# Queries and keys of a retention head projected by token, rotated there and turned by eight transposes

## The chip, the cores and the metric

The kernel runs on one core of a Trainium2 chip. The metric is the device time in microseconds of one execution, less is better. A core has a matrix engine (TensorE, in the profile PE, with its weight loads as PEld), a vector engine (VectorE, DVE), a scalar engine (ScalarE, ACT), GpSimd (POOL) and SyncE (SP), which here issues the DMAs. Matrix products are written to PSUM, of which the kernel uses eight banks of 128 partitions by 512 float32; everything else lies in SBUF.

## The reference

Two decoder layers over 256 tokens of width 2048, in float32. Each layer is a token mixer and a SwiGLU network, each with a root-mean-square norm, a shift and scale before it and a gate behind it that come from a conditioning vector through `w_mod`. The first layer's mixer is retention, the second's a short gated convolution. The change touches the retention alone:

```python
q, k, v, g = jnp.split(h @ w_in, [qk_w, 2 * qk_w, 2 * qk_w + v_w], axis=-1)
q = rope(split_heads(q, RET_HEADS), cos, sin)
k = rope(split_heads(k, RET_HEADS), cos, sin) * (RET_DK ** -0.5)
o = rms_norm(chunked_gated_linear_attention(q, k, v, log_a))
return ((jax.nn.silu(g) * o) @ w_out).astype(h.dtype)

def rope(t, cos, sin):
    half = t.shape[-1] // 2
    t1, t2 = t[..., :half], t[..., half:]
    return jnp.concatenate([t1 * cos - t2 * sin, t2 * cos + t1 * sin], axis=-1)
```

There are 8 heads. A head's queries and keys are 256 wide each, its values and its gate 512 each. The angle of `rope` is the token's position times one of 128 frequencies.

## The kernel before

**Precision.** Every float32 operand of a product is split into a high part, rounded to the matrix engine's faster float32 format, and a low part, the rest. A product is three matmuls: high by high, high by low, low by high. Weights come by DMA in pieces of 128 x 2048 (`fetch`, L291), of which each half of 1024 columns is rounded by ScalarE (L310) and subtracted by VectorE (L313). `laid_out` writes all weights into one array in the order in which the kernel uses them, and `take` hands them out in that order.

**Two forms of projection.** The hidden rows `h` lie transposed, 16 row tiles of 128 features by 256 tokens. In `packed` an item of 128 weight columns makes the weights stationary and streams the 256 tokens past them: three matmuls of 256 columns (L395 to L397), and the result has features on the partitions. An item of 512 columns goes to `by_token`: for each half of the tokens `h` is stationary and the 512 weight columns stream, three matmuls (L370 to L372), and the result has tokens on the partitions. Before the change q and k of a head are two items of 128 columns each, values and gate one item of 512. I call the work of one head and one row tile a step. A unit, by which `ticked` and `paced` count, is 128 weight columns of one row tile.

**The start.** While the modulation of the first norm is still coming in (32 loads of 1 MB, each reduced on VectorE, L656), q, k and gate are projected for five heads as far as rows of `h` are ready: `SPANS` lists the heads and row tiles, 60 steps in all. Two heads at a time fill the eight banks, and unfinished sums are put aside in SBUF (`held`, ScalarE L643 or VectorE L640). The last span, head 4, stays in its banks. In this part VectorE's and ScalarE's order is written by hand; the sines and cosines of the angles (`angles`) are made in between.

**The heads.** `projections` goes through the heads in the order 4, 0, 2, 1, 5, 3, 6, 7: the rest of q, its rotation on VectorE (`rope`, L822 to L826), the split into high and low (L828, L829), the same for k, then the values (`values`), the scores (`scores`, L857 and L860), the gate. What needs the scores is put on a list, `asides`, as pairs of a number of units and a piece of work: after 8 units of the next projection the first half of the outputs (L884), after 8 more the second half with its norm, after 20 more the eight transposes of the outputs (`ends`, L904), which turn them to features on partitions. The order on TensorE is the order in the program. On VectorE and ScalarE a scheduler orders the heads' work. `paced` lets go of the remaining modulation sums (L244, one pass of VectorE over 128 x 2048), after each group of projections up to two. In the middle and at the end of the heads stands a part of the output projection (`ret_out`).

**The norm behind.** The later norms read rows of `x`, scaled, from the same buffer as `h`, `raw_all`, with two columns more in front of each row for the shift (L528 to L530). Each row tile has a pitch of 514 columns there.

Of the kernel before, what the change touches and what calls it, by code (L numbers as in the profile page):

```python
# [10 lines left out]
F32 = mybir.dt.float32  # L11
F32R = mybir.dt.float32r
# [5 lines left out]
P = 128  # L18
# [26 lines left out]
MOD_PRIO = -300  # L45
STEPS = (8, 8, 20)
RAW_BUFS = 3
PART_BUFS = 4
LEFT, ENDS, EARLIER = 8, 2, 120

# [82 lines left out]
def in_use_order():  # L133

    for g in RET_SPANS:
        yield "ret_w_in", 0, g
    for n, h in enumerate(HEAD_ORDER):
        qkg, v = RET_HEADS[h]
        for g in qkg[:2] + [v] + qkg[2:]:
            yield "ret_w_in", 0, g  # L140
        if n % (HEADS // 2) == HEADS // 2 - 1:
            for g in RET_OUT[n // (HEADS // 2)]:
                yield "ret_w_out", 0, g
    for layer in range(DEPTH):
        if layer == 1:
            for g in CONV_IN:
                yield "conv_w_in", 0, g
            for g in CONV_OUT:
                yield "conv_w_out", 0, g
        for part in range(2):  # L150
            for g in FFN_IN[part]:
                yield "ffn_w_in", layer, g
            for g in FFN_OUT[part]:
                yield "ffn_w_out", layer, g


def laid_out(arrays):
# [4 lines left out]
    for key, i, g in in_use_order():  # L162
        for k in g.ks:
            for c, w in g.items:
                o = at % CHUNK
                out[at // CHUNK, :, o : o + w] = arrays[key][i, k * P : (k + 1) * P, c : c + w]
                at += w
    assert at == total and total % CHUNK == 0
# [7 lines left out]
def table():  # L176
# [9 lines left out]
def trunk(ctx: ExitStack, tc: tile.TileContext, x_in, c_in, pos_in, w_mod, cols_in, tab_in, w_all, out):  # L186
# [307 lines left out]
    h = rows_at(EARLIER)  # L494
    raw_all = h_all.rearrange("p (k n) -> p k n", k=KT + 1)[:, :KT, :]

    def scaled_only(layer, norm, j):

        needed(layer, SC2 if norm else SC1, j)
        a = mod_a[layer][norm][:, j : j + 1]  # L500
        high, low = raw_all[:, j, ENDS : ENDS + S], raw_all[:, j, ENDS + S :]
        nc.scalar.activation(high, x[j], AF.Identity, scale=a)
        nc.vector.scalar_tensor_tensor(low, x[j], a, high.bitcast(F32), op0=ALU.mult, op1=ALU.subtract)

    def normed(accs, layer, norm, g):
# [18 lines left out]
        for k in g.ks:  # L524
            high, low = raw_all[:, k, : ENDS + S], raw_all[:, k, ENDS + S :]
            for c, pt in zip(g.cols, banks):
# [53 lines left out]
    with ExitStack() as inner:  # L580
        rm = inner.enter_context(tc.tile_pool(name="rmid", bufs=1))

        def angles():

            both = rm.tile([P, 2, S], I32, tag="mid17", name=name("angles"))
            pos, ang = both[:, 0, :], both[:, 1, :].bitcast(F32)
            nc.sync.dma_start(pos, pos_in.to_broadcast([P, S]))
            magic = 1.5 * 2.0**23
# [8 lines left out]
            parts.append(rest)  # L597
            k = pos.bitcast(F32)
# [26 lines left out]
            ]  # L625

        sin = rm.tile([P, S], F32, tag="sin", name="sin")
        cos = rm.tile([P, S], F32, tag="cos", name="cos")
# [16 lines left out]
        with tc.tile_pool(name="start", bufs=1) as sp:  # L645
# [59 lines left out]
            with tc.manual_schedule(engines={mybir.EngineType.DVE, mybir.EngineType.Activation}):  # L705
# [6 lines left out]
                loaded(SH1, 0)  # L712
                nc.sync.dma_start(tab, tab_in[:, : 1 + P])
                fetch()
# [103 lines left out]

        def rope(s, tag, ours):

            a = tmp("qa", (P, 2, S), pool=rp, bufs=1)
            nc.vector.tensor_tensor(a, s, cos.unsqueeze(1).to_broadcast([P, 2, S]), op=ALU.mult)  # L822
            b = s if ours else tmp("qs", (P, 2, S), pool=rp, bufs=1)
            nc.vector.tensor_tensor(b, s, sin.unsqueeze(1).to_broadcast([P, 2, S]), op=ALU.mult)
            nc.vector.tensor_tensor(a[:, 0, :], a[:, 0, :], b[:, 1, :], op=ALU.subtract)
            nc.vector.tensor_tensor(a[:, 1, :], a[:, 1, :], b[:, 0, :], op=ALU.add)  # L826
            dst = rp.tile([P, 2, 2, S], F32R, tag=tag, name=name(tag))
            nc.scalar.copy(dst[:, 0, :, :], a)  # L828
            nc.vector.tensor_tensor(dst[:, 1, :, :], a, dst[:, 0, :, :].bitcast(F32), op=ALU.subtract)  # L829
            return dst  # L830

# [14 lines left out]

        def scores(head, q, k):
            decay = rp.tile([P, S], F32, tag="decay", name=name("decay"), bufs=1)
            nc.sync.dma_start(decay, tab_in[:, 1 + P + head * S : 1 + P + (head + 1) * S])
            both = []  # L850
            for jt in range(2):
# [16 lines left out]
                both.append(sp)  # L868
            return both

# [42 lines left out]

        def pair(head, i):

            g = RET_HEADS[head][0][i]
            if not g.ks:
                return [ahead[head, n] for n in ((i,) if i < 2 else (2, 3))]
            sums = packed(g, h)
            for j, pt in enumerate(sums):  # L920
                key = (head, i + j)
                if key in tag_of:
                    free.append(tag_of.pop(key))
                if key in ahead:
                    s = tmp("qs", (P, 2, S), pool=rp, bufs=1)
                    nc.vector.tensor_tensor(s, ahead[key], pt, op=ALU.add)
                    sums[j] = s
            return sums
# [150 lines left out]
```

## Time and profile before

| | us |
|---|---|
| median of the runs | 2627.57 (2622.59 to 2627.66) |
| the profiled execution | 2620.08 |
| its span, first to last instruction | 2618.3 |
| TensorE busy | 2592.6 |
| VectorE busy | 1991.1 |
| ScalarE busy | 1253.4 |
| first matmul of the projections | 19.43 |
| end of the spans | 202.27 |
| first part of the output projection | 348.87 |
| second part of the output projection | 686.87 |

A row of the groups reads: line, engine, operation, tile written <- tiles read, shapes, count, then busy time and mean duration of one, then the idle time of the engine before them and what ended it. A row of the timeline has the start and the duration of one instruction or of several alike. Matmuls overlap: the distance from one start to the next is what one costs, not the duration shown. A wait's row has the total in microseconds, how often, and the longest.

### The profile page before, as it was taken

How to read it: one execution, taken by the hardware profiler on the slowest of the kernel's cores; microseconds unless marked ns; L12 is line 12 of the kernel's file. 1: busy time of each engine (PE TensorE's matmuls, PEld its weight loads, DVE VectorE, ACT ScalarE, POOL GpSimd, SP SyncE). 2: the span in 40 equal slices, each digit the busy share in tenths (PEclk: the TensorE clock that was granted, in tenths of full speed). 3: DMA queues.
4: the chain of work that ended last, by engine and by line, in shares of the span. 5: the costliest groups of instructions: out<-in, count | busy, mean ns of one | idle time of the engine just before them, and what ended most of it. 6: DMA issues, size and time to landing. Idle time of an engine off the chain costs nothing.

```text
span 2618.3 us, 38264 instructions
## 1 busy us (share of the span) xinstructions
PE 2592.6 (99%) x15248; PEld 2305.3 (88%) x15248; DVE 1991.1 (76%) x2528; ACT 1253.4 (48%) x1791; POOL 141.8 (5%) x225
## 2 busy tenths in 40 slices
PE   7999999999999999999999999999999999999998
PEld 6898889888899888888888898888998888888888
DVE  7988878887698877777777889888887665555554
ACT  5544543444456444344444454444554443444443
POOL 0000000110000010110100001100000000000000
PEclk9999999999999999999999999999999999999999
DMA  9976668777686877777777768777677665555553
GB/s 397 390 288 224 250 250 304 291 260 275 243 306 247 329 290 278 270 287 289 288 267 281 272 224 324 288 277 270 256 272 267 251 224 193 192 186 186 192 193 129
DMA packets 96375, 687.58 MB, mean 263 GB/s; under 512 B 10690, under 2 KB 12098, under 8 KB 13250
## 3 DMA queue, kind: packets, MB, share of 16 engines
q1 hardware_dynamic: 96194, 685.13, 70.6%
q8 instruction: 119, 1.95, 0.3%
q14 instruction: 62, 0.50, 0.1%
HBM read 682.99 MB, written 2.10 MB: 262 GB/s over the span
## 4 chain that ended last, share of the span: by engine, by line
PE 75%; issue 20%; DVE 2%; DMA 2%; ACT 1%; DVEq 0%; POOLq 0%; POOL 0%; ACTq 0%
PE bank L355 34%; PE bank L358 18%; PE bank L370 4%; PE bank L371 4%; PE bank L372 4%; PE bank L397 2%; PE bank L396 2%; PE bank L395 2%; PE bank L528 1%; PE bank L530 1%; PE bank L529 1%; DMA raw<-w_all 1%; DVE raw L656 1%; DVE lo L313 1%; PE bank L884 1%
## 5 line engine op out<-in xcount | busy, mean ns | idle before, releaser
L313 DVE TENSOR_TENSOR lo<-raw,hi 128x1024 fp32r<-128x1024 f32 x912 | 1112.0, 1222 | 539.9 <-ACT hi L310 538.2
L310 ACT CAST hi<-raw 128x1024 fp32r<-128x1024 f32 x912 | 953.8, 1050 | 1075.6 <-PE bank L355 633.2
L355 PE MATMUL bank<-h,hi 128*128 128x512 f32 x3296 | 1142.9, 390 | 0.0
L358 PE MATMUL bank<-h,lo 128*128 128x256 f32 x3296 | 929.6, 282 | 0.0
L355 PEld LDWEIGHTS bank<-h,hi 128*128 128x128 f32 x3296 | 618.8, 188 | 129.5
L358 PEld LDWEIGHTS bank<-h,lo 128*128 128x128 f32 x3296 | 622.9, 189 | 0.2 <-DVE lo L313 0.2
L355 PE MATMUL bank<-mid,hi 128*128 128x512 f32 x1604 | 556.3, 390 | 0.0
L358 PE MATMUL bank<-mid,lo 128*128 128x256 f32 x1604 | 452.4, 282 | 0.3 <-DVE lo L313 0.3
L244 DVE SCALAR_TENSOR_TENSOR raw<-raw,cb 128x2048 f32<-128x2048 f32 x160 | 365.5, 2284 | 17.6 <-DMA raw<-w_mod 17.3
L355 PEld LDWEIGHTS bank<-mid,hi 128*128 128x128 f32 x1604 | 301.2, 188 | 63.1
L358 PEld LDWEIGHTS bank<-mid,lo 128*128 128x128 f32 x1604 | 303.2, 189 | 0.6 <-DVE lo L313 0.6
L370 PE MATMUL bank<-hi,h 128*128 128x512 f32 x512 | 201.6, 394 | 1.5 <-DVE rm L640 1.5
L371 PE MATMUL bank<-lo,h 128*128 128x512 f32 x512 | 200.4, 391 | 0.0
L372 PE MATMUL bank<-hi,h 128*128 128x512 f32 x512 | 199.6, 390 | 0.0
L355 PE MATMUL bank<-rm,hi 128*128 128x512 f32 x496 | 172.5, 390 | 0.0
L397 PE MATMUL bank<-h,lo 128*128 128x256 f32 x512 | 146.5, 286 | 4.3 <-DVE lo L313 4.3
L395 PE MATMUL bank<-h,hi 128*128 128x256 f32 x512 | 145.8, 285 | 3.3 <-ACT h L684 3.3
L396 PE MATMUL bank<-h,hi 128*128 128x256 f32 x512 | 146.0, 285 | 0.8 <-DVE h L685 0.8
L358 PE MATMUL bank<-rm,lo 128*128 128x256 f32 x496 | 139.8, 282 | 0.0
L372 PEld LDWEIGHTS bank<-hi,h 128*128 128x128 f32 x512 | 96.4, 188 | 20.7
L370 PEld LDWEIGHTS bank<-hi,h 128*128 128x128 f32 x512 | 96.8, 189 | 19.8 <-DVE rm L640 2.1
L371 PEld LDWEIGHTS bank<-lo,h 128*128 128x128 f32 x512 | 96.8, 189 | 17.3
(155 smaller groups left out, 2249.8 us busy)
## 6 DMA issues: line engine op xcount, KB each, us to landing
raw<-w_all SPq DMA_DIRECT2D x456, 1024.0 KB, 4.8
raw<-w_mod SPq DMA_DIRECT2D x192, 1024.0 KB, 5.0
x<-x_in SPq DMA_DIRECT2D x4, 512.0 KB, 5.7
out<-y SPq DMA_DIRECT2D x3, 512.0 KB, 3.6
decay<-tab_in SPq DMA_DIRECT2D x8, 128.0 KB, 3.2
out<-y SPq DMA_DIRECT2D x2, 256.0 KB, 4.5
cols<-cols_in SPq DMA_DIRECT2D x1, 160.0 KB, 8.9
angles<-pos_in SPq DMA_DIRECT2D x1, 128.0 KB, 9.6
```

The costliest lines, as they stand in the source:

```text
L244: nc.vector.scalar_tensor_tensor(raw, raw, 1.0, cb, op0=ALU.mult, op1=ALU.mult, accum_out=total)
L310: nc.scalar.copy(hi, raw)
L313: nc.vector.tensor_tensor(lo, raw, hi.bitcast(F32), op=ALU.subtract)
L355: nc.tensor.matmul(pt, hi, h, start=fresh and k == g.ks[0], stop=False, skip_group_check=True)
L358: nc.tensor.matmul(pt[:, 1, :], lo, h[:, 0, :], start=False, stop=last and k == g.ks[-1], skip_group_check=True)
L370: nc.tensor.matmul(o, ht[:, 0, :], hi, start=first, stop=False)
L371: nc.tensor.matmul(o, ht[:, 0, :], lo, start=False, stop=False)
L372: nc.tensor.matmul(o, ht[:, 1, :], hi, start=False, stop=last)
L395: nc.tensor.matmul(pt, hi, h[:, 0, :], start=first, stop=False, skip_group_check=True)
L396: nc.tensor.matmul(pt, hi, h[:, 1, :], start=False, stop=False, skip_group_check=True)
L397: nc.tensor.matmul(pt, lo, h[:, 0, :], start=False, stop=last, skip_group_check=True)
L528: nc.tensor.matmul(pt, hi, high, start=k == 0, stop=False, skip_group_check=True)
```

## The change

q and k of a head become one item of 512 columns, gathered from two places of `w_in`, so `packed` projects them through `by_token` and their tokens lie on the partitions. The rotation is done there, one call for each half of the tokens, with sines and cosines that have tokens on the partitions too; the angles are now made from the position as a scalar of each partition and a table with the frequencies in every row. Eight transposes (`turned_qk`) bring q and k of both halves into two banks with features on the partitions, where they are split as before. The turns and the scores become pieces of work on the list: the turns 32 units into the values (counted together with what is left on the list of the head before, at least 8), the scores 20 units behind them. The group of q and group of k become one, so `paced` is called once with 64 units for 2 x 32. The pitch of the rows in `raw_all` becomes 520. The rotated tile has two buffers.

```diff
+TURN_AT, SCORES_AT = 32, 20
-LEFT, ENDS, EARLIER = 8, 2, 120
+LEFT, ENDS, EARLIER, ROW = 8, 2, 120, 520
...
-        q = [Q0 + h * DK + i * P for i in range(2)]
-        k = [K0 + h * DK + i * P for i in range(2)]
-        qkg.append([q, k, [(G0 + h * DV, DV)]])
+        qkg.append([[((Q0 + h * DK, K0 + h * DK), 2 * DK)], [(G0 + h * DV, DV)]])
...
-    parts = [inv[:, None], np.eye(P), decay.transpose(1, 0, 2).reshape(P, HEADS * S)]
+    parts = [np.tile(inv, (P, 1)), np.eye(P), decay.transpose(1, 0, 2).reshape(P, HEADS * S)]
...
-    tab = const.tile([P, 1 + P], F32, tag="tab", name="tab")
-    inv_freq, ident = tab[:, 0:1], tab[:, 1 : 1 + P]
+    tab = const.tile([P, 2 * P], F32, tag="tab", name="tab")
+    inv_freq, ident = tab[:, :P], tab[:, P:]
...
-    h_all = hpool.tile([P, (KT + 1) * (ENDS + 2 * S)], F32R, tag="h", name="h")
-    hpool.tile([P, 88], F32, tag="beside", name="beside")
+    h_all = hpool.tile([P, KT * ROW], F32R, tag="h", name="h")
...
-            nc.sync.dma_start(pos, pos_in.to_broadcast([P, S]))
+            nc.sync.dma_start(pos, pos_in)
...
-                nc.vector.tensor_copy(ang, pos)
-                nc.vector.tensor_scalar(ang, ang, inv_freq, None, op0=ALU.mult)
+                nc.vector.tensor_copy(place, pos)
+                for t in range(2):
+                    at = slice(t * P, (t + 1) * P)
+                    nc.vector.tensor_scalar(ang[:, at], inv_freq, place[:, t : t + 1], None, op0=ALU.mult)
...
-        def rope(s, tag, ours):
-
-            a = tmp("qa", (P, 2, S), pool=rp, bufs=1)
-            nc.vector.tensor_tensor(a, s, cos.unsqueeze(1).to_broadcast([P, 2, S]), op=ALU.mult)
+        def rope(s, t, ours):
...
+            def whole(v):
+                return v[:, t * P : (t + 1) * P].unsqueeze(1).to_broadcast([P, 4, P])
...
+            a = tmp("qa", (P, 2, S), pool=rp, bufs=2)
+            nc.vector.tensor_tensor(parts(a), parts(s), whole(cos), op=ALU.mult)
             b = s if ours else tmp("qs", (P, 2, S), pool=rp, bufs=1)
...
+            nc.vector.tensor_tensor(parts(b), parts(s), whole(sin), op=ALU.mult)
+            (a0, a1), (b0, b1) = halves(a), halves(b)
+            nc.vector.tensor_tensor(a0, a0, b1, op=ALU.subtract)
+            nc.vector.tensor_tensor(a1, a1, b0, op=ALU.add)
+            return a
+
+        def turned_qk(both, q_and_k):
+
+            banks = [bank() for _ in range(2)]
+            for t, a in enumerate(both):
+                for n, pt in enumerate(banks):
+                    for i in range(2):
+                        nc.tensor.transpose(
+                            pt[:, i, t * P : (t + 1) * P], a[:, n, i * P : (i + 1) * P], ident
+                        )
+            for tag, pt in zip("qk", banks):
+                dst = rp.tile([P, 2, 2, S], F32R, tag=tag, name=name(tag))
+                nc.scalar.copy(dst[:, 0, :, :], pt)
+                nc.vector.tensor_tensor(dst[:, 1, :, :], pt, dst[:, 0, :, :].bitcast(F32), op=ALU.subtract)
+                q_and_k.append(dst)
...
         def projections(head):
-            q = rope(*pair(head, 0), "q", (head, 0) in ahead)
-            k = rope(*pair(head, 1), "k", (head, 1) in ahead)
+            both = pair(head, 0, rope)
+            waiting = sum(n for n, _ in asides) - since[0] if asides else 0
+            if not asides:
+                since[0] = 0
+            q_and_k, sp = [], []
+            asides.append((max(TURN_AT - waiting, STEPS[0]), lambda: turned_qk(both, q_and_k)))
+            asides.append((SCORES_AT, lambda: scores(head, *q_and_k, sp)))
             v = values(head, RET_HEADS[head][1])
-            sp = scores(head, q, k)
-            sg = [gate(s) for s in pair(head, 2)]
+            sg = pair(head, 1, lambda s, t, ours: gate(s))
+            if not asides:
+                since[0] = 0
             asides.extend(mixed(head, sp, v, sg))
-            since[0] = 0
```

More of the change, by code (lines that the diff above doesn't have):

```diff
@@ L138, in in_use_order @@
         qkg, v = RET_HEADS[h]
-        for g in qkg[:2] + [v] + qkg[2:]:
+        for g in qkg[:1] + [v] + qkg[1:]:
             yield "ret_w_in", 0, g
@@ L164, in laid_out @@
             for c, w in g.items:
-                o = at % CHUNK
-                out[at // CHUNK, :, o : o + w] = arrays[key][i, k * P : (k + 1) * P, c : c + w]
-                at += w
+                places = c if isinstance(c, tuple) else (c,)
+                for c in places:
+                    n, o = w // len(places), at % CHUNK
+                    out[at // CHUNK, :, o : o + n] = arrays[key][i, k * P : (k + 1) * P, c : c + n]
+                    at += n
     assert at == total and total % CHUNK == 0
@@ L625, in angles @@
             ]
+        pos = const.tile([P, 2], I32, tag="pos", name="pos")
+        place = const.tile([P, 2], F32, tag="place", name="place")
         sin = rm.tile([P, S], F32, tag="sin", name="sin")
@@ L712, in trunk @@
                 loaded(SH1, 0)
-                nc.sync.dma_start(tab, tab_in[:, : 1 + P])
+                nc.sync.dma_start(tab, tab_in[:, : 2 * P])
                 fetch()
@@ L845, in values, with scores @@
             return v
-        def scores(head, q, k):
+        def scores(head, q, k, both):
             decay = rp.tile([P, S], F32, tag="decay", name=name("decay"), bufs=1)
-            nc.sync.dma_start(decay, tab_in[:, 1 + P + head * S : 1 + P + (head + 1) * S])
-            both = []
+            nc.sync.dma_start(decay, tab_in[:, 2 * P + head * S : 2 * P + (head + 1) * S])
             for jt in range(2):
@@ L912, in mixed, with pair @@
             return list(zip(STEPS, [lambda: outputs(0), last_outputs, ends]))
-        def pair(head, i):
+        def pair(head, i, then):
             g = RET_HEADS[head][0][i]
+            keys = [(head, 2 * i + t) for t in range(2)]
             if not g.ks:
[L918 to L921, printed above, removed]
+                return [then(ahead[key], t, True) for t, key in enumerate(keys)]
+            out = []
+            for t, (key, pt) in enumerate(zip(keys, packed(g, h))):
+                s = pt
                 if key in tag_of:
```

29 lines of the change are left out of this document (12 added, 17 removed).

## The prediction

> **What bounds the kernel now.** I read the page's busy table and slices, then TensorE's waits, then busy time by stage, then the timeline where the two forms of projection stand side by side.
>
> ```profile
> span 2618.3 us, 38264 instructions
> PE 2592.6 (99%) x15248; PEld 2305.3 (88%) x15248; DVE 1991.1 (76%) x2528; ACT 1253.4 (48%) x1791; POOL 141.8 (5%) x225
> ...
> PEclk9999999999999999999999999999999999999999
> ```
>
> TensorE has work for 99% of the span at full granted clock. So what counts is how many matmuls it gets, how far apart they start, and where it waits; of that last there is little:
>
> ```profile
> PE bank L397 <- DVE lo L313: 4.3, 5, 1.8
> PE bank L395 <- ACT h L684: 3.3, 2, 2.5
> ...
> PE bank L370 <- DVE rm L640: 1.5, 2, 0.8
> ...
> PE bank L884 <- DVE sp L413: 0.5, 1, 0.5
> ```
>
> All but the last are in the first 128 us. By stage (columns: length, busy time and count of PE, PEld, DVE, ACT, POOL, granted clock, DMA share, GB/s):
>
> ```profile
> 19.00:128.00 109.00, 101.37 (x609) 89.80 (x609) 99.72 (x102) 61.43 (x93) 0.00 (x0) 0.98 1.00 406
> 128.00:203.00 75.00, 74.85 (x475) 67.92 (x476) 64.72 (x78) 36.66 (x49) 0.00 (x0) 1.00 0.74 279
> 225.10:687.00 461.90, 461.31 (x2586) 404.57 (x2586) 371.95 (x464) 209.07 (x285) 42.82 (x62) 1.00 0.73 267
> ```
>
> Up to 128 us the DMA engines are full (1.00) and VectorE is busy 91%, so TensorE is fed as fast as weights come and are split. From 128 us it is the bound. The stretch ends in a wait for VectorE's L640, part of an unbroken row of VectorE work:
>
> ```profile
> 127.42 0.68 DVE L640 TENSOR_TENSOR rm<-rm,bank 128x512 f32<-128x512 f32 x1
> 128.02 2.28 DVE L656 SCALAR_TENSOR_TENSOR raw<-raw,cb 128x2048 f32<-128x2048 f32 x1
> ```
>
> ```profile
> 128.15 0.50 PE L370 MATMUL bank<-hi,h 128*128 128x512 f32 x1 [0.77 <-DVE rm L640]
> ...
> 128.95 0.28 PE L395 MATMUL bank<-h,hi 128*128 128x256 f32 x1
> ...
> 199.45 0.28 PE L395 MATMUL bank<-h,hi 128*128 128x256 f32 x1
> ...
> 200.88 0.40 PE L370 MATMUL bank<-hi,h 128*128 128x512 f32 x1
> ...
> 202.27 0.39 PE L370 MATMUL bank<-hi,h 128*128 128x512 f32 x1
> ...
> 440.59 0.28 PE L395 MATMUL bank<-h,hi 128*128 128x256 f32 x1
> ...
> 463.61 0.40 PE L370 MATMUL bank<-hi,h 128*128 128x512 f32 x1
> ...
> 485.42 0.39 PE L857 MATMUL bank<-q,k 128*128 128x512 f32 x1
> ```
>
> From 440.59 to 463.61 stand 192 q and k matmuls of 256 columns (16 row tiles x 12), 119.9 ns apart; from 463.61 to 485.42 stand 96 of 512 columns (values), 227.2 ns apart. Twice 119.9 is 239.8: the same columns in half as many instructions cost 12.6 ns less a pair. From 128.95 to 202.27 stand 26 steps of one head and one row tile (12 narrow, 6 wide): 73.32/26 = 2.820 us each.
>
> **The change part by part.** *q and k by token.* A step's 12 narrow matmuls become 6 wide ones. In the spans 18 become 12 x 227.2 = 2.726 us, 0.094 us less. Of the 60 span steps 34 lie before 128 us; I count nothing for them, because TensorE, once faster, waits there longer for the DMA, the splitting L313 and L640, and 128.15 stays. After that 26 x 0.094 = 2.4 us. The heads' own 68 steps (6+6+4+4+3x16) save 12 x 119.9 - 6 x 227.2 = 76 ns each: 5.2 us. Together 7.6 us.
>
> *Eight transposes a head*, 64 in all, new on TensorE. They have the form of the output turns, L904, in the middle of a wide stream:
>
> ```profile
> 316.82 0.40 PE L370 MATMUL bank<-hi,h 128*128 128x512 f32 x1
> ...
> 320.93 1.03 PE L904 MATMUL bank<-tab,o 128*128 128x128 f32 x8
> 321.72 0.47 PE L370 MATMUL bank<-hi,h 128*128 128x512 f32 x1
> ...
> 339.53 0.39 PE L857 MATMUL bank<-q,k 128*128 128x512 f32 x1
> ```
>
> The eight take 0.79 us to the next start; the whole, 96 wide matmuls with the eight inside, takes 22.71 instead of 96 x 0.2272 = 21.81, so 0.90 us a head and 7.2 us for eight. The ends are 0.79 x 8 = 6.3 and 7.2; I take 7.2, which includes how the stream picks up again.
>
> *The head with nothing left to project* (head 4). Now its scores stand behind its values and its first output 24 matmuls later, too soon:
>
> ```profile
> 225.14 0.33 PE L395 MATMUL bank<-h,hi 128*128 128x256 f32 x1
> ...
> 228.29 0.73 PE L884 MATMUL bank<-v,sp 128*128 128x512 f32 x2
> 229.53 0.50 PE L884 MATMUL bank<-v,sp 128*128 128x512 f32 x1 [0.50 <-DVE sp L413]
> 229.86 0.28 PE L395 MATMUL bank<-h,hi 128*128 128x256 f32 x1
> ```
>
> 24 x 119.9 is 2.88 of the 3.15 us, and three outputs at 0.23 are 0.69 of 1.57: 1.15 us are lost. From the scores' end to the late matmul VectorE and ScalarE take 4.4 us. In the changed order 30 wide matmuls (6.8 us) lie between, so I take 0.9 of it back (ends 0 and 1.15).
>
> *Rotation, scores and the queues.* The rotation keeps its kinds and sizes on VectorE; the split of q and k reads a bank instead of SBUF:
>
> ```profile
> L313 DVE TENSOR_TENSOR lo<-raw,hi 128x1024 fp32r<-128x1024 f32 x912 | 1112.0, 1222 | 539.9 <-ACT hi L310 538.2 <-PE bank L397 0.2
> ...
> L244 DVE SCALAR_TENSOR_TENSOR raw<-raw,cb 128x2048 f32<-128x2048 f32 x160 | 365.5, 2284 | 17.6 <-DMA raw<-w_mod 17.3
> ...
> L413 DVE TENSOR_TENSOR rm<-bank,rm 128x256 fp32r<-128x256 f32 x32 | 12.3, 416 | 0.3
> ...
> L926 DVE TENSOR_TENSOR qs<-rm,bank 128x512 f32<-128x512 f32 x16 | 10.9, 679 | 0.7 <-PE bank L397 0.7
> ...
> L844 DVE TENSOR_TENSOR v<-bank,v 128x512 fp32r<-128x512 f32 x16 | 10.7, 685 | 2.5 <-ACT v L843 2.5
> ...
> L825 DVE TENSOR_TENSOR qa<-qa,qs 128x256 f32<-128x256 f32 x14 | 5.9, 421 | 0.2
> ...
> L822 DVE TENSOR_TENSOR qa<-bank,cos 128x512 f32<-128x512 f32 x8 | 5.5, 684 | 0.7 <-PE bank L397 0.7
> ...
> L828 ACT CAST q<-qa 128x512 fp32r<-128x512 f32 x8 | 4.9, 619 | 7.9 <-DVE qa L826 7.9
> ```
>
> A split out of a bank (L844) takes 685 ns, and a product that reads a bank (L822) 684: a bank costs VectorE no more. Access in pieces of 128 columns is not in the trace; its bounds are these rows and, far off, twice them. All of it hides behind the values' matmuls: the turns stand after 8 value rows, 8 x 6 x 0.2272 = 10.9 us after the projection ends. The tightest heads (0 and 1) queue on VectorE in that time 2 x (679 + 2 x 684 + 2 x 421) = 5.8 us of adding and rotating, three L313 of 1.22 and four pieces of 0.42 (L413) for the previous head's ends, 11.2 us, against 10.9 + 0.9 (those ends' own turns come first) = 11.8. The cover there is 0.6 us; the whole heads 5, 3, 6, 7 need 2 x (2 x 684 + 2 x 421) = 4.4 and two L313, 6.9 together, against 10.9. So no wait, but little to spare; without cover each late microsecond is TensorE's, since the turns stop everything behind them. The scores follow 20 units (6.8 us) after the turns, more than two copies of 619 ns (L828) and two splits of 685. The decay load keeps its place on SP one head ahead; SP and POOL issue as many instructions as before. The modulation sums L244 are let loose 2 at a time after the joint projection instead of 1 after q and 1 after k: the same number, in other places.
>
> *Loads and layout.* Positions shrink from 128 KB to 1 KB, the table grows from 64.5 to 128:
>
> ```profile
> angles<-pos_in SPq DMA_DIRECT2D x1, 128.0 KB, 9.6
> tab<-tab_in SPq DMA_DIRECT2D x1, 64.5 KB
> ```
>
> At 406 GB/s that is -0.31 + 0.16 = -0.15 us in a stretch where the DMA is full; ends -0.31 and +0.16. The rows of 520 instead of 514 columns, from which L528 to L530 read, change no count; ends -1 and +1 us (864 matmuls, 1 ns either way, the scatter of neighbours in the wide stream), taken as 0.
>
> *Sum.* -2.4 - 5.2 + 7.2 - 0.9 - 0.15 = -1.45 us. The profiled execution took 2620.08 us (span 2618.3 and 1.8 around it), so 2618.6. It lies 7.5 us under the median 2627.57, near the lowest run (2622.59); taken off the median it is 2626.1.
>
> **A rule against the row.** 227.2 ns for 512 columns and 119.9 for 256 make 0.419 ns a column and 12.6 ns that each matmul costs whatever its width. The Trainium skill, TensorE: Matmul & The Clock Gate, section Back-to-back issue gap, gives a warm gap of N/2.4 + 2.5 ns. By that page the fixed part is 2.5 ns, and a step would save only 6 x 2.5 = 15 ns where the rows give 76. Rows and rule disagree here, and the sum goes by the rows.
>
> **The rivals.**
> *The saving per matmul does not come (slower by about 0.2%).* What the narrow form loses might follow the stream it stands in rather than its width. The spans give a hint: in the step from 199.45 the 12 narrow ones take 1.43 us and the 6 wide ones, from 200.88 to 202.27, 1.39 us, 231.7 each. With 231.7 for the new ones a step saves 1.43 - 1.39 = 0.04 us, 94 steps 3.8, and the sum is 7.2 - 3.8 - 0.9 - 0.15 = +2.4 us; with no saving of the fixed part at all it is +7.2 - 0.9 - 0.15 = +6.2 us (2633.7). Against it: 96 wide ones in a row take 21.81 us. By the skill's rule above (15 ns, 94 steps, 1.4 us) the sum would be +4.8 us, 2632.4.
> *Rotation comes late (slower).* Both token tiles of q and k arrive together, so 4.4 to 5.8 us of rotation queue at once where before they came in two halves. If one L244 more (2.28 us) falls ahead of them in heads 0 and 1, the 0.6 us of cover is gone and TensorE waits 1.5 us and more at the turns or at L313's next piece. It decides from 0.85 us a head (6.7 us over eight); at 1.5 us a head the sum is +10.5, 2638. For it: the thin cover; against it: VectorE is busy 372 of 462 us in that stage and runs ahead.
> *The early stretch gains too (faster).* If TensorE's pace counts before 128 us, 34 x 0.094 = 3.2 us come on top, and with turns at 0.79 another 0.9: -5.5 us, 2622. For it: TensorE waits only 10 of those 109 us. Against it: DMA share 1.00 and the unbroken VectorE row up to 128.02.
>
> **How the numbers follow.** About 0.2% (5.2 us) is what a measurement of this kernel can tell from no change. Forecast 0.55, within it. No saving 0.10, half of it past the bound. Late rotation 0.15, slower. Early gain 0.20, three quarters past the bound. So faster 0.15, same 0.65, slower 0.20. The forecast's own range, from the ends of its terms (-0.9 for the turns, +0.9 and -0.25 for head 4, layout and loads +-1) and the scatter of the runs, is 2620 to 2629; with the rivals 2617 to 2634, which leaves out the worst of late rotation.
>
> **What the changed profile would show.** 64 more transposes and no narrow q and k matmuls, 1536 - 768 - 64 = 704 matmuls fewer; wide ones 227 ns apart in q and k; 0.9 us for each group of turns; no wait at head 4's first outputs; TensorE leaving its last wait for L640 near 128 us and head 4's projections ending some 2.4 us earlier relative to it; nothing changed after the retention. Wrong it would be if waits for the rotated tiles or for L313 appear between 225 and 687 us, if the wide stream runs at 231 ns, or if the L640 wait comes clearly before 128 us.

## The result, and the profile after

The changed kernel takes 2628.87 us (median of 22 runs, 2625.64 to 2633.06), the kernel before 2622.84 (22 runs, 2619.93 to 2627.66): a ratio of 1.0021, 95% interval 1.0014 to 1.0027, so some 5.5 us slower. The profiled execution took 2625.87 us against 2620.08, its span 2623.8 against 2618.3. The forecast was 1.45 us less than before, counted as no change.

The busy table of the kernel after, and the first three rows of TensorE's waits:

```profile
span 2623.8 us, 36863 instructions
PE 2591.7 (99%) x14544; PEld 2271.9 (87%) x14544; DVE 1991.1 (76%) x2529; ACT 1255.3 (48%) x1791; POOL 129.4 (5%) x225
```

```profile
PE bank L528 <- DVE h L515: 5.9, 1, 5.9
PE bank L372 <- DVE lo L314: 4.8, 5, 1.3
PE bank L371 <- ACT h L687: 3.5, 2, 2.6
```

TensorE has 704 matmuls fewer, as counted, and VectorE as much to do as before. One wait is new and the longest of all: the first matmul of the norm behind the retention (L528) waits 5.9 us for `ends[1]`, the low part of that norm's shift (L515). Neither line is in the retention; the change's edits there are the pitch of 520 and nothing else. TensorE's timeline around the wait, kernel after:

```profile
775.94 0.28 PE L398 MATMUL bank<-rm,lo 128*128 128x256 f32 x1
782.17 0.55 PE L528 MATMUL bank<-h,hi 128*128 128x258 f32 x1 [5.95 <-DVE h L515]
782.52 0.41 PE L529 MATMUL bank<-h,hi 128*128 128x256 f32 x1
782.74 0.42 PE L530 MATMUL bank<-h,lo 128*128 128x258 f32 x1
782.95 0.42 PE L528 MATMUL bank<-h,hi 128*128 128x258 f32 x1
```

From 775.94 to 782.17 are 6.23 us, where 0.12 would do: 6.1 lost. Before the change this L528 started at 778.64 without a wait. So TensorE reached it 2.6 us earlier and left it 3.5 us later. After it the matmuls stand 214 ns apart instead of 120. The stages show why (granted clock is the third column from the end; kernel before, then after):

```profile
782.00:790.00 8.00, 8.00 (x71) 8.00 (x70) 5.18 (x9) 4.14 (x7) 1.56 (x1) 1.00 0.79 284
790.00:1515.00 725.00, 725.00 (x4273) 646.39 (x4272) 565.78 (x691) 346.25 (x498) 53.18 (x81) 1.00 0.76 283
```

```profile
776.00:782.00 6.00, 0.22 (x2) 0.02 (x1) 5.97 (x11) 3.01 (x5) 0.56 (x2) 0.83 0.94 351
782.00:790.00 8.00, 7.83 (x49) 7.86 (x50) 2.54 (x4) 1.05 (x1) 0.09 (x1) 0.70 0.66 256
790.00:1515.00 725.00, 725.00 (x4272) 646.55 (x4271) 565.38 (x688) 346.21 (x495) 56.30 (x83) 1.00 0.75 282
```

The clock record holds a stretch at 0.50 there, from 779.98 to 786.80. The norm's stage, from its first L528 to the first L528 of the next norm, takes 737.06 us (782.17 to 1519.23) against 734.89 (778.64 to 1513.53): 2.2 us more, which e5 below puts down to the half clock. The balance of the two profiles: -2.6 to the end of the retention, +6.1 wait, +2.2 clock, and -0.2 in all that follows, +5.5.

Why is the shift late? VectorE's timeline, first after, then before:

```profile
769.36 2.28 DVE L245 SCALAR_TENSOR_TENSOR raw<-raw,cb 128x2048 f32<-128x2048 f32 x1
...
775.36 2.28 DVE L245 SCALAR_TENSOR_TENSOR raw<-raw,cb 128x2048 f32<-128x2048 f32 x1
...
777.57 0.48 DVE L565 SCALAR_TENSOR_TENSOR x<-bank,g,x 128x256 f32<-128x256 f32 x1
777.96 2.28 DVE L245 SCALAR_TENSOR_TENSOR raw<-raw,cb 128x2048 f32<-128x2048 f32 x1
...
781.84 0.18 DVE L515 TENSOR_TENSOR h<-s,h 128x16 fp32r<-128x16 f32 x1
```

```profile
772.03 2.28 DVE L244 SCALAR_TENSOR_TENSOR raw<-raw,cb 128x2048 f32<-128x2048 f32 x1
...
778.03 0.18 DVE L515 TENSOR_TENSOR h<-s,h 128x16 fp32r<-128x16 f32 x1
778.13 2.29 DVE L244 SCALAR_TENSOR_TENSOR raw<-raw,cb 128x2048 f32<-128x2048 f32 x1
```

L515 needs 48 modulation sums (16 rows of each of the first three kinds on the list). Before, the 48th is the one at 772.03, and L515 goes ahead of the next. After, the 48th is the one at 777.96, behind the last product of the output projection: `normed` had to call it in itself, by `needed`. `paced` had fallen behind. Counted through by its rule, it adds 0.045 a unit to an allowance with a cap of 2.0, and each sum takes 1.0. In a whole head (5, 6 or 7) it got 1.44 behind q and 1.44 behind k, and with what was left over it let go three sums behind q and k of head 5, three again in head 6 and two in head 7. Called once with 64 units, 2.88 is cut to 2.0: two. So one sum was lost in head 5 and one in head 6, 39 sums instead of 41 were out when the heads ended, and at the output projection's end 47 instead of 49.

The parts that the prediction priced, kernel after: a group of turns in the stream, the same in a whole head (head 5), and head 4's first outputs.

```profile
209.33 0.39 PE L373 MATMUL bank<-hi,h 128*128 128x512 f32 x1
209.56 1.03 PE L852 MATMUL bank<-tab,qa 128*128 128x128 f32 x8
210.35 0.48 PE L371 MATMUL bank<-hi,h 128*128 128x512 f32 x1
...
225.26 0.85 PE L911 MATMUL bank<-v,sp 128*128 128x512 f32 x3
...
471.03 1.03 PE L852 MATMUL bank<-tab,qa 128*128 128x128 f32 x8
471.82 0.48 PE L371 MATMUL bank<-hi,h 128*128 128x512 f32 x1
```

No turn waits, and no output of head 4. The 144 wide matmuls ahead of 471.03 (96 of q and k, 48 of the values) start at 438.37: 226.8 ns each.

The end of the early stretch, kernel after:

```profile
123.16 0.40 PE L373 MATMUL bank<-hi,h 128*128 128x512 f32 x1
125.40 0.49 PE L371 MATMUL bank<-hi,h 128*128 128x512 f32 x1 [1.84 <-DVE rm L643]
125.73 0.39 PE L372 MATMUL bank<-lo,h 128*128 128x512 f32 x1
125.96 0.40 PE L373 MATMUL bank<-hi,h 128*128 128x512 f32 x1
127.13 0.50 PE L371 MATMUL bank<-hi,h 128*128 128x512 f32 x1 [0.77 <-DVE rm L643]
```

The waits for the sums put aside, 0.69 and 0.77 us before, are now 1.84 and 0.77, and the last ends 1.0 us earlier than before (128.15). From start to start TensorE idles 2.24 us here. That turned out to matter.

### The profile page after: what moved, and what is told of

It is laid out like the page before. It is cut to its first block, busy times and chain, and to the rows that moved or that the text cites. A ratio compares the mean times of both kernels' runs of the same rounds, so it can differ in the third digit from the quotient of the medians.

```text
span 2623.8 us, 36863 instructions
## 1 busy us (share of the span) xinstructions
PE 2591.7 (99%) x14544; PEld 2271.9 (87%) x14544; DVE 1991.1 (76%) x2529; ACT 1255.3 (48%) x1791; POOL 129.4 (5%) x225
## 3 DMA queue, kind: packets, MB, share of 16 engines
q8 instruction: 113, 1.85, 0.3%
## 4 chain that ended last, share of the span: by engine, by line
PE 75%; issue 20%; DVE 2%; DMA 2%; ACT 0%; DVEq 0%; POOLq 0%; POOL 0%; ACTq 0%
PE bank L356 34%; PE bank L359 18%; PE bank L371 6%; PE bank L373 5%; PE bank L372 5%; DMA raw<-w_all 1%; PE bank L528 1%; PE bank L529 1%; PE bank L530 1%; DVE lo L314 1%; DVE raw L659 1%; DMA raw<-w_mod 1%; PE bank L911 1%; PE bank L727 0%; PE bank L852 0%
## 5 line engine op out<-in xcount | busy, mean ns | idle before, releaser
L314 DVE TENSOR_TENSOR lo<-raw,hi 128x1024 fp32r<-128x1024 f32 x912 | 1111.8, 1223 | 534.9 <-ACT hi L311 528.7
L359 PE MATMUL bank<-h,lo 128*128 128x256 f32 x3296 | 929.5, 282 | 0.0
L371 PE MATMUL bank<-hi,h 128*128 128x512 f32 x768 | 302.5, 394 | 6.1 <-ACT h L687 3.5
L372 PE MATMUL bank<-lo,h 128*128 128x512 f32 x768 | 301.3, 392 | 5.2 <-DVE lo L314 4.8
L373 PE MATMUL bank<-hi,h 128*128 128x512 f32 x768 | 300.5, 391 | 0.0
L372 PEld LDWEIGHTS bank<-lo,h 128*128 128x128 f32 x768 | 144.8, 188 | 39.3 <-DVE lo L314 10.1
L371 PEld LDWEIGHTS bank<-hi,h 128*128 128x128 f32 x768 | 144.9, 189 | 37.6 <-ACT h L687 4.2
L373 PEld LDWEIGHTS bank<-hi,h 128*128 128x128 f32 x768 | 144.7, 188 | 30.2
L356 PEld LDWEIGHTS bank<-rm,hi 128*128 128x128 f32 x496 | 93.1, 188 | 19.5
L359 PEld LDWEIGHTS bank<-rm,lo 128*128 128x128 f32 x496 | 93.7, 189 | 0.3
L406 ACT COPY low<-bank 128x256 f32<-128x256 f32 x222 | 80.5, 363 | 27.4 <-PE bank L359 16.2
```

The costliest lines, as they stand in the source:

```text
L314: nc.vector.tensor_tensor(lo, raw, hi.bitcast(F32), op=ALU.subtract)
L356: nc.tensor.matmul(pt, hi, h, start=fresh and k == g.ks[0], stop=False, skip_group_check=True)
L359: nc.tensor.matmul(pt[:, 1, :], lo, h[:, 0, :], start=False, stop=last and k == g.ks[-1], skip_group_check=True)
L371: nc.tensor.matmul(o, ht[:, 0, :], hi, start=first, stop=False)
L372: nc.tensor.matmul(o, ht[:, 0, :], lo, start=False, stop=False)
L373: nc.tensor.matmul(o, ht[:, 1, :], hi, start=False, stop=last)
```

## The experiments

The theory: pacing, not the rotation, makes the kernel slower, by a late shift and the half clock behind it. The rivals: the by-token form, turns or pitch cost that time (rival 2); VectorE is late at L515 whenever TensorE comes earlier (rival 3). Each kernel was timed beside the kernel before on the same chip: e1 to e4 on one, e5 to e8 on another, e9 to e11 on a third, so across these groups only the ratios compare. The times below are medians of 11 runs (5 for e2).

**e1, pacing put back.**

```diff
-        paced(g.n * len(g.ks))
+        joint = isinstance(g.items[0][0], tuple) and len(g.items) == 1
+        for _ in range(1 + joint):
+            paced(g.n * len(g.ks) // (1 + joint))
```

> The kernel after, but `paced` is called twice with 32 units behind the joint projection, as it was behind q and behind k; by token, turns and the pitch of 520 stay. Theory 1 (one call with 64 units runs into the cap of 2.0, two modulation sums fall behind, the last sum of the second norm's shift is forced late, TensorE waits 6.1 us for L515 and then runs about 7 us at half clock): the sum is in time again, L515 ends near 778 us as before the change; TensorE comes at 776, so a wait of 0 to 2 us is left, too short for the clock to fall. 2616.5 to 2618.5 in the profile's terms, -1.5 to -3.5 us against the kernel before, ratio 0.9987 to 0.9995. Rival 2 (the by-token form, the turns or the pitch of 520 cost what the result shows): stays at +5.5 us, ratio 1.002. Rival 3 (VectorE is late at L515 in any case because TensorE comes earlier): a wait of over 4 us stays, and the half clock with it, ratio 1.001 to 1.002.

Measured: 2622.35 us, ratio 1.0005 (0.9996 to 1.0014). The wait at L528 and the half clock there are gone: L517, the line that was L515, runs at 777.49, TensorE comes at 778.20. Rivals 2 and 3 fall. But by the ratio the kernel is 1.3 us over the one before where 1.5 to 3.5 under it were expected, and the trace shows two reasons. The first is behind head 5's joint projection, where three sums are let go at once again (VectorE and TensorE, e1):

```profile
462.99 2.29 DVE L245 SCALAR_TENSOR_TENSOR raw<-raw,cb 128x2048 f32<-128x2048 f32 x1
465.20 0.08 DVE L245 DVE_READ_ACCUMULATOR raw<-raw,cb 128x1 f32 x1
465.20 0.68 DVE L842 TENSOR_TENSOR qs<-bank,sin 128x512 f32<-128x512 f32 x1
465.80 1.21 DVE L314 TENSOR_TENSOR lo<-raw,hi 128x1024 fp32r<-128x1024 f32 x1
```

```profile
467.07 0.50 PE L372 MATMUL bank<-lo,h 128*128 128x512 f32 x1 [0.25 <-DVE lo L314]
```

A sum stands between the rotation's steps, the splitting L314 behind it is late, and compared matmul by matmul with the kernel after, TensorE loses 0.5 us at this place and 0.7 at the same place of head 6. The second reason is a half clock of 3.41 us from 125.60, which the profile after does not have; it costs 0.9 us.

**e2, the fault without the change.** The kernel before, with one call for q and k together:

```diff
-        paced(g.n * len(g.ks))
+        kept[0] += g.n * len(g.ks)
+        if g.n != 2 or len(kept) == 2:
+            paced(kept[0])
+            kept[:] = [0]
+        else:
+            kept.append(0)
```

> The kernel before, q and k in two narrow groups as they were, but the units of both are handed to `paced` in one call of 64 behind k. Nothing else is changed, no transposes, pitch 514. Theory 1: the same two modulation sums fall behind, the last sum for the shift is forced; TensorE comes at 778.64, the shift at about 781.8, so a wait of some 3.2 us at L528, and if the clock falls after that, 2 us more: +3 to +5.5 us against the kernel before, ratio 1.0012 to 1.0021. Rival 2: no change, ratio 1.000. Rival 3: no change beyond 1 us.

Measured: 2630.39 us, ratio 1.0034 (1.0021 to 1.0046). The narrow kernel becomes slower by more than the change made it (by the profiles 2.0 of its 11.3 us come in the early stretch):

```profile
780.56 0.28 PE L397 MATMUL bank<-rm,lo 128*128 128x256 f32 x1
787.35 0.55 PE L533 MATMUL bank<-h,hi 128*128 128x258 f32 x1 [6.51 <-DVE h L520]
```

So the calls to `paced` alone explain the new wait. The size was off. I had put the late shift at a fixed time, 781.8, so that TensorE, coming later, would wait only 3.2 us. It waits 6.5. In both profiles (after and e2) the row of VectorE work that L515's line closes is the same, two sums with the last product's line between them and some more, and it starts only as TensorE's last products do: the shift comes 5.9 us behind TensorE's last matmul in the kernel after, 6.5 in e2. The clock is at 0.50 from 784.88 to 791.70 and, in this kernel too, once in the early stretch (129.52 to 132.93).

**e3 and e4, the cap at 3.0**, in the kernel after and in the kernel before:

```diff
-        allowed[0] = min(allowed[0] + n * MOST, 2.0) if n <= 64 else 0.0
+        allowed[0] = min(allowed[0] + n * MOST, 3.0) if n <= 64 else 0.0
```

> The kernel after with one number changed: the cap of the allowance in `paced` is 3.0 instead of 2.0, so 64 units at 0.045 (2.88) are not cut off and the 48 sums that L515 needs are let go two groups of the output projection earlier than in the kernel before the change. Theory 1: no wait at L528 at all, no half clock: -2.6 us from the retention kept whole and some 0.3 behind it, about -3 us against the kernel before, ratio 0.9985 to 0.9993. Rival 2: +5.5 us. Rival 3: the wait is shorter but stays over 3 us, ratio 1.000 to 1.002.

> Control: the kernel before with the cap at 3.0. It has no wait for the shift to lose. Theory 1: no change, -0.5 to +0.5 us, ratio 0.9998 to 1.0002, and what e3_cap_3 is faster than this is the price of the change itself (-2 to -3.5 us). Rival 2: no change here either, but then e3_cap_3 is 5.5 us slower than this one. Rival 3: 0 to -1 us.

Measured: e3 2620.76 us, ratio 0.9997 (0.9988 to 1.0006); e4 2622.29, ratio 1.0004 (0.9995 to 1.0013). No wait at L528 in e3, L515 runs at 771.09, 6.7 us before TensorE comes; rivals 2 and 3 fall once more. e3 is 1.5 us under e4, short of the 2 to 3.5 that the theory said, and 0.8 us under the kernel before where 3 were expected. The shortfall in e3's profile is again the third sum behind head 5 (0.6 us against the kernel after) and a half clock, from 126.86 (1.6 us: 84.02 us from the last wait for the sums put aside to the first turn, where the kernel after needs 82.43). e4 too loses 1.1 us behind head 5 against the kernel before, at a wait for L313, though it lets go of no more sums there; what else sets it off is not shown.

**e5, the clock by itself.** The kernel after, kept busy during the wait:

```diff
                 (pt,) = packed(g, act, base)
+                if which == (0, GT1):
+                    busy = bank()
+                    for _ in range(56):
+                        nc.tensor.transpose(busy[:, 0, :P], ident, ident)
```

> The kernel after with 56 transposes of the identity into a bank that nothing reads, issued behind the last matmul of the second output projection, so that TensorE works (5.5 us of the 99 ns a turn takes) while it waits for L515. The wait itself stays. Theory (the wait costs 6.1 us, and another 2.2 us come from the clock, which the idle time lets fall to 0.50 for 6.8 us): L528 starts where it starts in the kernel after, the half clock there is gone, and L528 to L530 stand 120 ns apart from the start: 2.2 us less than after, +3.3 us against the kernel before, ratio 1.0013. Rival (the matmuls at the start of this stage are slow for another reason, such as weights split late or the new shift columns): no gain, ratio 1.002.

Measured: 2626.26 us, ratio 1.0015 (1.0006 to 1.0025), against 1.0021 of the kernel after. The stages of e5 to hold against those of after:

```profile
776.00:782.00 6.00, 6.00 (x56) 6.00 (x55) 6.00 (x7) 1.82 (x5) 0.19 (x1) 1.00 0.95 352
782.00:790.00 8.00, 8.00 (x72) 8.00 (x71) 4.81 (x10) 3.06 (x4) 0.37 (x1) 1.00 0.93 369
```

The 56 turns take 6.0 us (778.37 to 784.40), as long as the wait did, the clock stays at 1.00, and the norm's stage is back at 734.97 us (784.40 to 1519.37). So by the profiles 2.1 us of the 5.5 came from the clock, not from the wait, and the rival falls. The timed runs point the same way, but the intervals of the two ratios overlap.

**e6 and e7, the pacing held equal.** e6 is e3 with at most two sums a call; e7 has the same rule and e2's joint call in the narrow kernel:

```diff
-        while todo and n_mod - len(todo) < due and allowed[0] >= 1.0:
-            allowed[0] -= 1.0
-            modulation(*todo.pop())
+        for _ in range(2):
+            if todo and n_mod - len(todo) < due and allowed[0] >= 1.0:
+                allowed[0] -= 1.0
+                modulation(*todo.pop())
```

> The kernel after with the cap at 3.0, but at most two sums let go by one call. In e3 three sums came together behind the projection of the first whole head, and TensorE lost 1.3 us at L372 for the splitting L314 there (465.8 us). Theory: with two a call that wait is gone, 48 sums are still let go two groups early, no wait at L528, no half clock there: 1 us under e3, -1.5 to -2.6 us against the kernel before, ratio 0.9990 to 0.9994. Rival (the wait at 465.8 us comes from the joint rotation, not from the third sum): stays, ratio 0.9997.

> Control with the old narrow form: q and k in two groups as before, their 64 units handed to `paced` in one call, cap 3.0, at most two a call, so that every modulation sum is let go behind the same group as in e6. What e6 is faster than this is the price of by token, turns and layout with the pacing held equal. Theory (the sum of the prediction, -1.45 us, of which the retention shows -2.6 in the profile): this one is at 0 to +0.5 us against the kernel before, ratio 1.0000 to 1.0002, and e6 is 1.5 to 2.6 us faster. Rival (turns and rotation cost more than the wide form saves): this one is 1 us and more faster than e6.

Measured: e6 2620.81 us, ratio 0.9993 (0.9985 to 1.0002); e7 2620.63 us, ratio 0.9993 (0.9985 to 1.0002). No wait is left at 465 us in e6; the wait had cost 0.6 us and not the 1.3 of the expectation, which had taken a difference from the wrong start, and e6 and e3 cannot be told apart. e7 comes out lower than expected, though its interval reaches there, and with equal pacing the narrow kernel is as fast as e6, where e6 should have been 1.5 to 2.6 us ahead. So no gain of the by-token form can be measured here, although its matmuls save what they were to save. The early stretch shows what takes 1.6 us of it back (e6, then e7):

```profile
124.00:134.00 10.00, 8.04 (x27) 6.20 (x28) 8.97 (x12) 3.67 (x6) 0.00 (x0) 0.83 0.79 311
```

```profile
124.00:134.00 10.00, 8.57 (x54) 7.31 (x53) 10.00 (x12) 4.71 (x7) 0.00 (x0) 1.00 0.80 316
```

In e6 the clock is at 0.50 for 3.41 us right behind the waits of 1.85 and 0.77 us for the sums put aside (L643 in the kernel after). From the last of these waits to the first turn e6 needs 84.02 us (126.92 to 210.94), the kernel after, without that half clock, 82.43 (127.13 to 209.56): 1.6 us. Of the six by-token kernels whose waits at this place are untouched (after, e1, e3, e5, e6 and e8), five have the half clock there in their profile. Of the four narrow ones with theirs (before, e2, e4, e7), only e2 has it, whose first wait is 1.41 us instead of 0.5 to 0.7. Over the timed runs the mean granted clock is 0.9985 in e6 and 0.9991 in e7: 0.0006 of 2620 us are 1.6 us of clock, about one such stretch a run. But this mean holds every stretch at 0.50, also those near 27 us that five of the thirteen profiles have, and e10 below, without these waits, has 0.9987. So it does not show how often the clock falls at this place in the timed runs.

Why the kernel after was spared, the records show. In each run all edges of the stretches at 0.50 lie a whole number of steps of 3.41 us apart, and every fall follows a step in which TensorE was little busy (by the profile's rows, whose matmul ends are modelled). The step before e6's fall and the one behind it, then the kernel after's least busy step here:

```profile
123.45:126.86 3.41, 0.97 (x3) 0.48 (x3) 3.41 (x6) 0.00 (x0) 0.00 (x0) 1.00 0.54 226
126.86:130.27 3.41, 3.35 (x8) 2.67 (x9) 3.41 (x5) 1.63 (x4) 0.00 (x0) 0.50 0.81 286
```

```profile
124.62:128.03 3.41, 1.86 (x7) 1.25 (x8) 3.41 (x6) 0.00 (x0) 0.00 (x0) 1.00 0.61 195
```

The waits are the same, but in the kernel after the edge at 124.62 cuts the longer one in two, and no step is under 1.86 us busy (0.54). Over all thirteen profiles, from the first clock record on, every step at full clock with a busy share up to 0.49 is followed by one at 0.50, no step with 0.54 or more is, and between these both occur (0.53 in e2 is, 0.51 in e3 at 24.46 us is not). So it was the place of the steps that spared the profile after, by luck: its -2.6 us is the better case.

**e8, the turns' price.** e6 with every turn of q and k issued twice:

```diff
-            for t, a in enumerate(both):
+            for t, a in list(enumerate(both)) * 2:
```

> e6 with each of the 64 turns of q and k issued twice into the same place of the bank. It prices a group of eight in the stream: by the prediction 0.90 us a head with what the stream loses when it picks up again, 0.79 by start to start. Expected between +6.3 and +7.2 us against e6, so +4 to +5.5 us against the kernel before, ratio 1.0015 to 1.0021. If turns were cheaper in the stream than their distance (hidden behind weight loads or waits), under +3 us against e6; if the rotation's splits behind them have no cover and TensorE then waits for the scores, +10 us and more, with waits at L885.

Measured: 2628.04 us, ratio 1.0019 (1.0010 to 1.0028), 7.2 us over e6: 0.90 us a group.

```profile
211.52 1.91 PE L853 MATMUL bank<-tab,qa 128*128 128x128 f32 x16
213.19 0.48 PE L372 MATMUL bank<-hi,h 128*128 128x512 f32 x1
```

Sixteen take 1.67 us to the next start, eight took 0.79: the added ones cost 0.88, since turns stand 109 ns apart and the matmul behind the last one starts 0.03 us after it. The splits behind them keep their cover; no wait at the scores. One group of turns does wait, head 1's, 0.54 us for the rotated tile.

**e9, e10 and e11, the early half clock.** e9 is e6 with work in the first of the two waits:

```diff
+                if g is RET_SPANS[3] and k == g.ks[0] and i == 3:
+                    o = banks[5].rearrange("p a b -> p (a b)")
+                    for _ in range(6):
+                        nc.tensor.matmul(o, h[:, 0, P:], zeros[0], start=False, stop=False, skip_group_check=True)
```

> e6 with six matmuls of 512 columns against a tile of zeros, added to a sum that TensorE has just begun, in the place where it waits 1.84 us for L643 (about 123 us): 1.36 us of work that changes no number, inside a wait that stays. Theory (the by-token kernels idle there 2.24 us from start to start where the narrow ones idle 1.2; in four of five of their profiles the clock falls to 0.50 for 3.41 us right behind it, their mean granted clock over the timed runs is 0.9985 against 0.9991, and that eats some 1.5 us of the 2.6 that the retention gained): no half clock near 127 us, mean clock 0.9990, 1.0 to 1.7 us under e6, ratio against the kernel before 0.9987 to 0.9990. Rival (the clock there is of no account, the price of the change is simply zero): as e6, ratio 0.9993, or up to 0.2 us more.

Measured: 2618.39 us, ratio 0.9985 (0.9976 to 0.9994), mean clock 0.9990. e6 had 0.9993. e9's timeline and stage:

```profile
123.90 1.56 PE L395 MATMUL bank<-zero,h 128*128 128x512 f32 x6
125.89 0.51 PE L373 MATMUL bank<-hi,h 128*128 128x512 f32 x1 [0.43 <-DVE rm L649]
```

```profile
124.00:134.00 10.00, 8.79 (x38) 6.60 (x37) 10.00 (x12) 3.68 (x6) 0.00 (x0) 1.00 0.75 301
```

TensorE leaves the waits no earlier (127.63, against 126.92 in e6), only the clock is different: from there to the first turn it needs 82.43 us where e6 needs 84.02, 1.6 us less. The step of 3.41 us that holds the first wait (123.30 to 126.71) is now 2.98 us busy. By this profile the rival, that the clock there is of no account, falls. By the ratios the kernel is some 2 us faster, in line, though their intervals overlap.

e10 and e11 take the wait away instead, in e6 and in e7:

```diff
-                            due.append((step[0] + 0.2 * (i - 4), lambda key=key, pt=pt: held(key, pt)))
+                            due.append((step[0] + 0.0 * (i - 4), lambda key=key, pt=pt: held(key, pt)))
```

> e6 with the four late sums of a span put aside at once instead of spread between the reductions of the next rows (the step 0.2 becomes 0.0), so that VectorE frees the last two banks ahead of the reduction of 2.28 us that TensorE now waits for at 123 us. Theory (as in e9): the idle time of 2.24 us shrinks below 1.2, the half clock behind it goes, and TensorE leaves the stretch up to 1.5 us earlier: -1 to -2.5 us against e6, ratio 0.9983 to 0.9990. Rival (VectorE is the bound of that stretch, the rows of h are then late by what the sums are early): the wait moves to the next row, no gain, ratio 0.9993.

> Control: the same edit of 0.2 to 0.0 in e7, the narrow form with the same pacing. There the waits at this place were 0.69 and 0.77 us and the clock did not fall. Theory: 0 to -0.7 us against e7, ratio 0.9990 to 0.9994, so the by-token kernel with this edit (e10) is 1 us and more faster than this one. Rival: this one gains as much as e10 does.

Measured: e10 2618.25 us, ratio 0.9983 (0.9974 to 0.9991), the lowest of all, though level with e9 and e11, and faster than both kernels; e11 2618.41 us, ratio 0.9987 (0.9978 to 0.9996). In e10 the waits for the sums put aside and the half clock near 127 us are gone:

```profile
124.00:134.00 10.00, 9.44 (x42) 7.46 (x41) 10.00 (x11) 5.24 (x8) 0.00 (x0) 1.00 0.73 289
```

But the narrow kernel gains from the edit as well, more than I had allowed it (2.1 us in its profile). In the timed runs its ratio falls by 0.0006 from e7's, e10's by 0.0010 from e6's, and each ratio is known to 0.0009 either way, so the rival of e11, that it gains as much, is not refuted. By the profiles e10 is ahead of e11 by 1.9 us when the second norm begins (from the first matmul of the projections, 774.14 - 18.92 against 776.41 - 19.25) and by 1.2 us at the end. In the timed runs the means of 11 differ by 0.55 us, with an uncertainty of 0.95. The price of by token itself, pacing and early waits held equal, thus lies between a gain of 1.5 us and a loss of 0.4; its sign is not settled.

## Why the prediction was wrong, step by step

- *Matmuls and their distance: right.* 704 fewer; q, k and values 226.8 ns apart, so a step saves 12 x 119.9 - 6 x 226.8 = 78 ns where 76 were forecast. The 231 ns of the first rival did not come, in the spans neither (226.7 from 127.93 to the first turn).
- *Turns: right.* 0.79 us to the next start, 0.90 with what the stream loses after them, and 7.2 us for 64 more by e8.
- *Head 4: right.* Three outputs in 0.69 us (225.26 to 225.94) without a wait, where they took 1.57.
- *Late rotation: it did not come.* No turn waits in the kernel after. Its mechanism is real, though: in e1 and e3 one sum more behind head 5 made TensorE wait for the splitting L314, at 0.5 and 0.6 us, and in e8 the turns of head 1, one of the two heads with the thinnest cover, wait 0.54 us. (The prediction counts head 3 as a whole head; by its own list of steps it has four rows left, and 5, 6 and 7 are whole.)
- *Pitch and loads: right at nothing.* The norm's stage is 734.89 us with 514 columns and 734.97 in e5 with 520; the first matmul starts at 19.43 before, at 19.39 after.
- *"TensorE, once faster, waits there longer ... and 128.15 stays": half right.* It waits longer and leaves 1.0 us earlier, in this profile (0.2 to 1.1 in the six by-token kernels with these waits, each from its first matmul of the projections). The step stopped at the wait and did not ask what a longer one does to the clock: 1.6 us in e6. The prediction read "full granted clock" off the slices, but its own table has 0.98 for 19 to 128 us: the kernel before has a stretch at 0.50 from 27.26 to 30.67. It cost nothing, for TensorE is not the bound there: the last wait ends 108.72 us after the first matmul of the projections, and in e7, without that stretch, 108.75.
- *"The same number, in other places": the step that failed.* The modulation sums let go are not the same number. I had counted two for one and one, and not carried the allowance through its cap over all heads; it comes out two sums short, one in head 5 and one in head 6. The last one for the shift is late, and TensorE waits 6.1 us and then loses 2.2 by the clock (e2 has this without the change, e1, e3 and e6 have the change without this). *"Nothing changed after the retention"* fell with it.

The sum for the retention was -1.45 us; the profile after shows -2.6 to its end, of which 1.0 is the early stretch's earlier end. From the last early wait to the retention's end it is -1.6 (650.5 us before, 648.9 after), so the terms there were right in size too, in a profile that the half clock spared. The sign of the whole was lost outside the functions that the matmuls are counted in.

The Trainium skill, TensorE: Matmul & The Clock Gate, Part 1: The HAM clock gate, says that the clock falls to half after an idle window of about 3.4 us and rises after as long a busy one, in a window that runs free of the kernel. The 3.41 us and 6.83 us at 0.50 agree with one and two such windows, and the edges that lie whole steps of 3.41 us apart agree with a window that runs free. That a whole idle window is needed does not agree: here waits of 1.84 and 0.77 us, with matmuls between them, were enough in five profiles of six, with TensorE busy for 0.28 to 0.46 of the window before the fall, and the measurement decides.

## What to carry to other kernels

Where background work is paced by calls with a size, merging two calls is a change of the pacing: run its counter over the whole kernel before and after, and look for the first place that forces what is missing. TensorE, busy 99% here, paid for a wait twice, once by the wait and again by the clock behind it, so a stage that gets faster ahead of a fixed release can lose what it gained; a little useless work in the gap, or a release moved forward, is worth trying. Compare a change with a control whose pacing is the same, or the experiment prices the schedule and not the change.

## What the runs showed of the hardware that I had not expected

A wait of 6.1 us brought the clock to 0.50 for 6.83 us, a pair of waits of 1.84 and 0.77 us to 0.50 for 3.41 us (0.9 us lost in e1, 1.5 to 1.6 in e3, e5, e6 and e8) in five kernels and not in the sixth. The step of 3.41 us before told whether it fell: up to 0.49 busy it always did, from 0.54 on never, and e9, which fills that step, has no fall there. Near 27 us, where TensorE is not the bound, the same stretch at 0.50 cost nothing (before against e7). Turns of an identity into a bank that nothing reads, and matmuls that add zeros, hold it at 1.00 (e5, e9). At half clock a matmul of 256 columns takes 214 ns instead of 120, not 240.
